# A log-sum-exp kernel on one core: six large loads issued in halves from two queues

## The chip, the cores and the metric

The kernel runs on one core of a Trainium2 chip. The metric is the device time of one execution in microseconds (us). The time before the change is the median of three runs, 162.56 us (162.5 to 163.04).

## What is computed

The input is a float32 array of 32 x 512 x 1024 numbers, normally distributed. For each of the 16384 rows of 1024 numbers the logarithm of the sum of the exponentials is taken, which leaves 32 x 512 numbers.

```python
def reference(x: np.ndarray, axis: int) -> np.ndarray:
    x_max = np.max(x, axis=axis, keepdims=True)
    return (x_max.squeeze(axis) + np.log(np.sum(np.exp(x - x_max), axis=axis))).astype(np.float32)
```

The kernel takes no maximum off: it computes log(sum(exp(x))) directly. The input is 67.1 MB, the output 64 KB.

## The kernel before

The 16384 rows are laid over the 128 partitions, 128 consecutive rows to each partition (`x_v`, L51). What a partition holds is worked off in 17 chunks of 4, 15, 16, 16, 16, 14, 13, 9, 7, 5, 4, 3, 2, 1, 1, 1 and 1 rows (`CHUNKS`, L11). A row of a partition is 4 KB, so a load of chunk 1 brings 60 KB into each of 128 partitions, and a load of chunks 2, 3 and 4 brings 64 KB.

The chunks land in a ring of 51 rows per partition (`ring`, L54). Chunks 0 to 3 fill it exactly (4 + 15 + 16 + 16). Chunk 4 starts at the front again, over chunks 0 and 1; chunk 5 lies over the end of chunk 1 and most of chunk 2; chunk 6 over the end of chunk 2 and the first half of chunk 3; chunk 7 over the first half of chunk 4, and so on.

All loads are issued by SyncE in the order of the chunks (`load`, L92 to L102). Ahead of a load that goes over used rows, SyncE waits until VectorE (`dve_done`) and, where needed, ScalarE (`act_done`) have finished with them. Chunk i has a semaphore of its own, `landed[i]`, which its load raises by 16. The load of chunk 0 is moved ahead of the first barrier (L184 to L192).

ScalarE works in the order of the program. It loads its table (L122); for every chunk it waits for `landed[i]` (L135), and takes Exp in place in one or two parts (L137). VectorE sums each part along its rows as soon as that Exp is done, with one reduction (L157), or row by row with a fused add of the row's two halves in chunks 8, 9, 10 and 12 (L144). In some chunks the last row, and in chunks 13 to 16 the only row, is summed by ScalarE itself while it takes Exp (L164). The logarithms are taken by ScalarE in three instructions (L108): for the first 81 rows per partition ahead of chunk 7, for the next 43 rows ahead of the last chunk's row, and for the last four at the end. Each waits for the sums that it reads. SyncE then stores the result (L176).

No scheduler orders the work: the order on each engine is that of the program text.

The softmax here doesn't subtract the row's maximum and nothing guards it: scores larger than these inputs give would overflow.

## Time and profile before

| what | value |
|---|---|
| median of three runs | 162.56 us |
| the profiled execution's own time | 162.84 us |
| span of its profile | 161.5 us |
| VectorE busy | 121.0 us (75% of the span) |
| ScalarE busy | 115.1 us (71%) |
| DMA packets' time, as a share of 16 engines' span | 97.3% |
| read from memory | 67.11 MB, mean 416 GB/s over the span |
| ScalarE's idle time until a load has landed | 43.9 us in 7 waits |
| VectorE's idle time until an Exp is done | 37.2 us in 4 waits |

The landings follow from the starts of ScalarE's Exps that waited for a load: chunk 0 at 7.44 us from the span's start, chunk 1 at 25.65, chunk 2 at 45.33, chunk 3 at 64.81, chunk 4 at 84.14, chunk 5 at 101.07 and chunk 6 at 116.83. After that ScalarE hardly waits. The span begins with SyncE's first issue, and the profiled execution's time is 1.3 us longer than its span. All numbers that are read from the profile are of that one execution.

To read the lines below: DVE is VectorE, ACT is ScalarE, SP (or SPq, its queue) is SyncE; L157 is line 157 of the kernel. A line of a timeline gives start and duration in us, engine, line, operation, output and input with their shapes, how many instructions were merged, and in brackets the idle time before the first and what ended it.

### The profile page before, as it was taken

The page shows a single profiled execution, that of the slowest core. Times are in us where ns is not written, and L with a number is a line of the kernel's source. Part 1 is how long each engine was busy: PE and PEld are TensorE (multiplying, and loading weights), DVE is VectorE, ACT ScalarE, POOL GpSimd, SP SyncE. Part 2 cuts the span into 40 slices and gives each one's busy share as a digit, 9 for nine tenths or more (in the row PEclk, how much of TensorE's full clock was granted, in tenths as well). Part 3 has the DMA queues.
Part 4 walks back from the last instruction along what each step waited for, and adds up shares of the span by engine and source line. Part 5 has one row for each costly group of instructions (what it writes and reads, how often), then busy time and mean ns, then how long its engine had stood idle before and what let it go on. Part 6 is the DMA issues. An engine that isn't in the chain of part 4 may idle for free.

```text
span 161.5 us, 126 instructions
## 1 busy us (share of the span) xinstructions
DVE 121.0 (75%) x46; ACT 115.1 (71%) x40; POOL 0.2 (0%) x4
## 2 busy tenths in 40 slices
DVE  0028000004999999999999599999999999999892
ACT  3170006995079960999519993999199999999995
POOL 0000000000000000000000000000000000000000
DMA  7999899989799799699799999999899999999991
GB/s 268 495 487 457 350 411 520 406 373 520 308 471 520 325 455 520 276 503 520 325 422 455 455 455 438 422 422 422 366 429 438 444 433 406 441 414 423 405 407 36
DMA packets 2592, 67.18 MB, mean 416 GB/s; under 512 B 288, under 2 KB 416, under 8 KB 928
## 3 DMA queue, kind: packets, MB, share of 16 engines
q1 hardware_dynamic: 2592, 67.18, 97.3%
HBM read 67.11 MB, written 0.07 MB: 416 GB/s over the span
## 4 chain that ended last, share of the span: by engine, by line
DMA 49%; DVE 29%; ACT 20%; issue 0%
DMA ring<-in_x_dram 49%; DVE sums L157 29%; ACT ring L137 17%; ACT ring L164 3%; ACT res L108 0%
## 5 line engine op out<-in xcount | busy, mean ns | idle before, releaser
L157 DVE TENSOR_REDUCE sums<-ring 128x8 f32<-128x8192 f32 (+5 forms) x14 | 111.2, 7995 | 37.4 <-ACT ring L137 37.2
L137 ACT ACTIVATE ring<-ring 128x8192 f32<-128x8192 f32 (+6 forms) x18 | 104.4, 5836 | 44.0 <-DMA ring<-in_x_dram 43.9
L144 DVE CUSTOM_DVE_ANT_0 ring<-ring 128x512 f32<-128x512 f32 x16 | 9.9, 688 | 0.0
L164 ACT ACTIVATE ring<-ring 128x1024 f32<-128x1024 f32 x9 | 9.3, 1042 | 0.0
L122 ACT ACT_TABLE_LOAD x1 | 1.3, 1283 | 0.8 <-PEq L209 0.8
L164 ACT ACTIVATION_READ_ACCUMULATOR ring<-ring 128x1 f32 x9 | 1.6, 173 | 0.0
L144 DVE DVE_READ_ACCUMULATOR2_ANT sums<- 128x1 f32 x16 | 1.4, 85 | 0.0
L108 ACT ACTIVATE res<-sums 128x81 f32<-128x81 f32 (+1 forms) x2 | 0.5, 248 | 0.0
L108 ACT ACTIVATE res<-late 128x4 f32<-128x4 f32 x1 | 0.2, 173 | 0.0
L209 POOL MEMSET const-bfloat16-1.0<- 128x1 bf16 x1 | 0.1, 102 | 0.0
L209 POOL MEMSET const-uint8-127<- 128x1 uint8 x1 | 0.1, 102 | 0.0
L209 POOL MEMSET const-float32-0.0<- 128x1 f32 x1 | 0.1, 99 | 0.2 <-issue 0.2
L209 POOL MEMSET const-float32-1.0<- 128x1 f32 x1 | 0.1, 99 | 0.0
## 6 DMA issues: line engine op xcount, KB each, us to landing
ring<-in_x_dram SPq DMA_DIRECT2D x1, 7680.0 KB, 24.8
ring<-in_x_dram SPq DMA_DIRECT2D x1, 7168.0 KB, 29.0
ring<-in_x_dram SPq DMA_DIRECT2D x1, 6656.0 KB, 36.2
ring<-in_x_dram SPq DMA_DIRECT2D x1, 4608.0 KB, 20.3
ring<-in_x_dram SPq DMA_DIRECT2D x2, 2048.0 KB, 16.1
ring<-in_x_dram SPq DMA_DIRECT2D x1, 3584.0 KB, 28.4
ring<-in_x_dram SPq DMA_DIRECT2D x1, 2560.0 KB, 27.4
ring<-in_x_dram SPq DMA_DIRECT2D x4, 512.0 KB, 27.1
```

Source lines behind the costliest of these rows:

```text
L108: nc.scalar.activation(out=res[:, lo:hi], in_=src, func=Ln).then_inc(act_done, 1)
L122: nc.scalar.preload_act_table_set("natural_log_exp_and_others")
L137: nc.scalar.activation(out=ring[:, s + lo : s + hi], in_=ring[:, s + lo : s + hi], func=Exp).then_inc(act_done, 1)
L144: nc.vector.tensor_tensor_reduce(out=ring[:, s + j, : D // 2], in0=ring[:, s + j, : D // 2], in1=ring[:, s + j, D // 2 :], scale=1.0, scal ...
L157: nc.vector.reduce_sum(out=sums[:, row + lo : row + hi], in_=ring[:, s + lo : s + hi], axis=AX).then_inc(dve_done, 1)
L164: nc.scalar.activation(out=ring[:, s + j], in_=ring[:, s + j], func=Exp, accum_out=total(row + j),).then_inc(act_done, 1)
L209: nc = _bacc.Bacc("TRN2", target_bir_lowering=False, num_devices=1)
```

## The change

Chunks 1 to 6 (`TWO_QUEUES`) are loaded by two transfers each: SyncE issues the 64 even partitions, ScalarE the 64 odd ones. A partition's piece is as large as before and contiguous as before. Both raise the chunk's semaphore by 16, so ScalarE waits for 32. The loads of chunk 0 and of chunks 7 to 16 stay whole on SyncE.

On ScalarE the three odd halves of chunks 1 to 3 are issued at the start, ahead of the table load. The odd half of chunk 4 is issued behind the Exps of chunk 2, that of chunk 5 behind those of chunk 3, and that of chunk 6 behind those of chunk 4. ScalarE makes the same waits ahead of them as SyncE makes ahead of the even halves: for chunk 4 on the sum of chunk 1, for chunk 5 on the second sum of chunk 2, for chunk 6 on the first sum of chunk 3. SyncE's order of loads is unchanged.

```diff
+TWO_QUEUES = range(1, 7)
...
-    def load(i):
+    def fetch(engine, i, first=0, step=1):
         (s, row), r = place[i], CHUNKS[i][0]
         act_wait = max(a for a, _ in busy[s : s + r])
         dve_wait = max(d for _, d in busy[s : s + r])
         if dve_wait:
-            nc.sync.wait_ge(dve_done, dve_wait)
+            engine.wait_ge(dve_done, dve_wait)
         if act_wait:
-            nc.sync.wait_ge(act_done, act_wait)
-        nc.sync.dma_start(out=ring[:, s : s + r], in_=x_v[:, row : row + r]).then_inc(
-            landed[i], 16
-        )
+            engine.wait_ge(act_done, act_wait)
+        engine.dma_start(
+            out=ring[first:P:step, s : s + r], in_=x_v[first:P:step, row : row + r]
+        ).then_inc(landed[i], 16)
+
+    def load(i):
+        if i in TWO_QUEUES:
+            fetch(nc.sync, i, 0, 2)
+        else:
+            fetch(nc.sync, i)
...
+    for i in range(1, 4):
+        fetch(nc.scalar, i, 1, 2)
     nc.scalar.preload_act_table_set("natural_log_exp_and_others")
...
-        nc.scalar.wait_ge(landed[i], 16)
+        nc.scalar.wait_ge(landed[i], 32 if i in TWO_QUEUES else 16)
...
         done_before.append((dves, acts))
+        if i + 2 in TWO_QUEUES and i + 2 > 3:
+            fetch(nc.scalar, i + 2, 1, 2)
```

## The prediction, made before the changed kernel was run

> **What bounds the kernel now.** I read the page first (engine shares, the 40 slices), then the busy time by stretch, then the two compute engines' timelines, then SyncE's waits and issues.

> ```profile
> DVE  0028000004999999999999599999999999999892
> DMA  7999899989799799699799999999899999999991
> q1 hardware_dynamic: 2592, 67.18, 97.3%
> DMA packets 2592, 67.18 MB, mean 416 GB/s; under 512 B 288, under 2 KB 416, under 8 KB 928
> ```

> One queue carries everything, and its 16 DMA engines are hardly ever without work. The packet counts give the descriptor: 17 loads of 128 partitions are 2176 packets, the store is 128, and 288 under 512 B are 18 transfers times 16 completion writes; the sum is 2592. So a packet here is one partition's row of one load (15 x 4 KB = 60 KB in load 1, 64 KB in loads 2 to 4), and each engine has 8 of them per load. The mean rate hides nothing in the middle. A line of the next view is a stretch, its length, busy DVE, ACT, POOL, the clock, the DMA share and GB/s; I cut at the landings of loads 0 to 6.

> ```profile
> 7.44:25.65 18.21, 4.42 (x1) 3.62 (x2) 0.00 (x0) 1.00 1.02 435
> 25.65:45.33 19.68, 6.65 (x1) 13.01 (x2) 0.00 (x0) 1.00 1.00 426
> 45.33:64.81 19.48, 19.48 (x3) 13.94 (x2) 0.00 (x0) 1.00 1.00 431
> 64.81:84.14 19.33, 19.33 (x3) 13.95 (x3) 0.00 (x0) 1.00 0.99 427
> 116.83:159.86 43.03, 40.39 (x37) 42.88 (x27) 0.00 (x0) 1.00 0.94 401
> ```

> Two facts. The DMA already moves 426 to 435 GB/s through the large loads, with a share of 0.99 to 1.02. And in the last 43 us ACT is busy 42.88: from load 6's landing at 116.83 ACT is the bound too, with the transfers ending just ahead of it (the last lands at 158.5, its Exp starts at 158.56). VectorE is the third limit:

> ```profile
> 11.09 4.42 DVE L157 TENSOR_REDUCE sums<-ring 128x4 f32<-128x4096 f32 x1 [11.09 <-ACT ring L137]
> 38.68 50.52 DVE L157 TENSOR_REDUCE sums<-ring 128x15 f32<-128x15360 f32 x5 [23.18 <-ACT ring L137]
> 91.20 53.00 DVE L157 TENSOR_REDUCE sums<-ring 128x8 f32<-128x8192 f32 x7 [1.99 <-ACT ring L137]
> ...
> 153.75 3.35 DVE L157 TENSOR_REDUCE sums<-ring 128x3 f32<-128x3072 f32 x1 [0.97 <-ACT ring L137]
> ```

> From 38.68 us, when load 1's sum starts, VectorE has only two gaps until its last sum at 158.3: 1.99 and 0.97 us. The end then follows ScalarE's L108 (waits for those sums), one row and one L108, to 159.86. Load 1's landing at 25.65 sets the start: 13.0 us of Exp, then 38.68. So a later load 1 has 2.0 + 1.0 us of free play, plus some 0.1 at the end, together 3.1 us, and beyond that the end moves one for one. SyncE's side is looser:

> ```profile
> SPq L100 <- DVE sums L157: 123.0, 7, 52.4
> 54.86 0.33 SPq L100 DMA_DIRECT2D ring<-in_x_dram  x1
> ```

> Load 4 is issued at 54.86, 9.95 us before load 3 has landed (64.81); an issue takes 0.33 us.

> [...] The trace has one queue; its issues take 0.33 to 0.75 us, so there is next to nothing to save. [...] No trace here shows two busy queues; this is the step on which my number rests. [...]

> **The change, part by part.** Instructions: ScalarE gains six DMA issues (three ahead of its table load, one each behind the Exps of chunks 2, 3 and 4) and three waits on sums; SyncE keeps 17 issues. Six issues at 0.33 to 0.75 us are 2 to 4.5 us of ScalarE's sequencer. The first three fall in the 5.38 us that ACT idles before load 0; the others ahead of waits of 5.38, 2.80 and 3.51 us for loads 4, 5 and 6. Cost nothing; without that cover 0.33 us each. No issue falls in the ACT-bound last 43 us.

> The bytes do not change, nor the descriptors. The gain has a ceiling: loads 2 and 3 took 19.68 and 19.48 us against 18.21 x 16/15 = 19.42 at load 1's rate, so perfect overlap of two queues returns some 0.3 us over the large loads; below nothing, the same amount could be lost in switching. I take 0.

> What moves is the order of packets. Before, load 0's 8 rows per engine go first, then load 1's 8. Now ScalarE's queue offers load 1's odd rows from about the first barrier on (SyncE's second issue is at 0.78; the first packets ran 1.0 us after the first issue, so 1.8 at the earliest), then those of loads 2 and 3, with nothing to hold them back. If an engine alternates packet by packet, every 16 KB row of load 0 left over is followed by a 60 or 64 KB row that is not yet needed. Costs: a 60 KB row is 18.21/8 = 2.28 us, a 64 KB row about 19.6/8 = 2.45, a 16 KB row 2.28 x 16/60 = 0.61. Load 0's last row ended near 7.0 before. ScalarE's rows join with n of load 0's rows left: n = 7 if they come at 1.8, n = 4 if they take some 1.5 to 2 us longer. I take 6, since an engine's first row started at 1.0 to 1.9 and takes over 0.6 us at the start.
> - Load 0: 7.0 + 4 x 2.28 + 2 x 2.45 = 21.0. Its Exp and sum (3.6 and 4.4 us) have time until load 1.
> - Load 1's even rows alternate with four 64 KB rows: 4 x (2.28 + 2.45) = 18.9, so 39.9, and landed about 40.2: 14.5 us later than 25.65.
> - VectorE starts load 1's sum at 40.2 + 13.0 = 53.2 and is then never short of work, since loads 2 and 3 still land near 54 and 65 (the sum of bytes is the same). It ends 14.5 - 3.1 = 11.4 us later.
> - The waits: load 4's both halves need load 1's sum, done at 53.2 + 16.2 = 69.4, while the DMA runs dry at 64.8: some 5 to 6 us of empty DMA, and load 4 lands near 90. ScalarE waits in line for that sum too (behind Exp of chunk 2, ending near 68.5) and then holds chunk 3's Exp for 1 us; behind chunk 3 it waits for chunk 2's second sum (53.2 + 16.2 + 17.3 = 86.7), ahead of load 4's landing. Queued behind it are only Exps whose sums VectorE reaches later. ACT's last stretch then starts 6 us late, inside VectorE's 11.4.
> Sum: 162.84 (this execution's own time; span 161.5) + 11.4 = 174.2; its own time stands 0.28 above the median 162.56, so about 174.0. With n = 4, load 1 lands 9.8 us late: +6.7, 169.2. With n = 7: 17.0 late, +13.9, 176.5.

> **The rivals.**
> 1. Fair sharing by bytes. If an engine mixes both queues finely, n = 6 rows of load 0 take twice 6 x 0.61, landing 3.7 us later, and ScalarE's queue stays 1.6 MB (3.7 us) ahead. Load 1 lands 3.3 to 4 us late; after the 3.1 us of play the end moves 0.2 to 0.9: about 163.1. For it: the slices show even flow. Against: the records are whole rows, one after the other.
> 2. Not slower: whole shares. An engine stays with one transfer's rows until its completion write, then changes queue. [...] Then load 0 is finished first, odd and even of load 1 follow, and all six landings stand: 162.6, or 162.3 with the 0.3 us gained. It decides from the point where load 1 lands by 28.7 (25.65 + 3.1). Against it: the profile counts each row as a packet.
> 3. [...] the six loads (109.4 us from 7.44 to 116.83) could take up to twice that: some 270. [...]
> 4. The change doing little because the later three halves come late from ScalarE: load 6's odd half is issued only behind chunk 4's Exps. It is still ahead of load 5's landing, so nothing by itself.

> **How the numbers follow.** Packet by packet 0.57; bytes 0.17; whole shares 0.14; a small gain 0.04; [...] another loss 0.04. The forecast is 174.0. What a measurement of this kernel can tell from no change is about 0.3% (0.5 us). Half of the byte case falls within it: same 0.14 + 0.08, slower 0.57 + 0.09 + 0.04 + 0.04, faster 0.04. The likeliest case alone spans 168.5 to 177; to leave out less than 2 in 10 the range must take in bytes and whole shares: 162.4 to 177. [...]

> **What would show it.** Right: ACT's first Exp starts near 21 instead of 7.44, its second near 40; VectorE's 128x15 sum starts near 53 and runs without a gap to about 170; load 4 is issued near 69 with an empty slice in the DMA row; GB/s elsewhere near 430. Wrong: load 1 landed by 29 (rivals 1, 2), or GB/s near 220 in the first slices (rival 3), or a gap in VectorE after load 1.

## The result, and the profile after

The changed kernel took 169.07 us (168.94 to 169.26, four runs) against 162.66 us (162.5 to 163.04, four runs) for the kernel before: a ratio of 1.039, 95% interval 1.037 to 1.041. It is slower by 6.4 us. The forecast was 174.0 with a range of 162.4 to 177.0. The profiled execution took 169.06 us with a span of 167.7, against 162.84 and 161.5 before.

The page of the changed kernel, lines of the 40 slices and of the DMA queues:

```profile
DVE  0000180000049999999999999999999999999992
DMA  7989998998999797699989999999899999999920
q1 hardware_dynamic: 2208, 43.58, 61.5%
q10 hardware_dynamic: 480, 23.59, 32.6%
```

There are two queues now. ScalarE's (q10) carries six transfers of 64 rows and 16 completion writes each (records of 4 bytes, as many to a transfer as the page counts DMA engines), 6 x 80 = 480 packets, so a packet is still one partition's row, or one such write. VectorE's row is the one that changed: its run of nines starts two slices later, then has no weak spot, and goes on to the end, while the DMA row has already fallen to 2 and 0.

Three stretches of the same kernel: between the landings of loads 0 and 1, between those of loads 1 and 2, and from load 6's landing on (stretch, length, busy DVE, ACT, POOL, clock, DMA share, GB/s):

```profile
16.49:35.24 18.75, 4.42 (x1) 3.62 (x2) 0.00 (x0) 1.00 1.01 437
35.24:54.68 19.44, 6.41 (x1) 13.00 (x1) 0.00 (x0) 1.00 1.01 432
119.91:166.08 46.17, 44.63 (x38) 42.99 (x27) 0.00 (x0) 1.00 0.88 372
```

While both queues have rows the rate is 437 and 432 GB/s, as with one queue (435 and 426 before). So the bytes flow as before; what they belong to has changed. And in the last stretch VectorE, not ScalarE, is busy nearly throughout.

The timeline of the changed kernel shows what became late; ahead of it stands the line of the kernel before for load 1:

```profile
25.65 13.00 ACT L137 ACTIVATE ring<-ring 128x15360 f32<-128x15360 f32 x1 [14.59 <-DMA ring<-in_x_dram]
```

```profile
0.78 2.27 ACTq L102 DMA_DIRECT2D ring<-in_x_dram  x3
16.49 3.62 ACT L149 ACTIVATE ring<-ring 128x4096 f32<-128x4096 f32 x1 [12.12 <-DMA ring<-in_x_dram]
35.24 13.00 ACT L149 ACTIVATE ring<-ring 128x15360 f32<-128x15360 f32 x1 [15.13 <-DMA ring<-in_x_dram]
48.27 103.21 DVE L169 TENSOR_REDUCE sums<-ring 128x15 f32<-128x15360 f32 x12 [23.72 <-ACT ring L149]
54.68 13.95 ACT L149 ACTIVATE ring<-ring 128x8192 f32<-128x8192 f32 x2 [6.45 <-DMA ring<-in_x_dram]
64.46 0.50 ACTq L102 DMA_DIRECT2D ring<-in_x_dram  x1
87.22 7.03 ACT L149 ACTIVATE ring<-ring 128x8192 f32<-128x8192 f32 x1 [4.75 <-DMA ring<-in_x_dram]
```

Load 0 lands at 16.49 instead of 7.44, load 1 at 35.24 instead of 25.65, load 2 at 54.68 instead of 45.33. Load 3 is complete at 64.57 by its semaphore, in time: the same bytes have arrived by then, but those of load 3 were mixed in among those of loads 0 to 2. VectorE's 128x15 sum starts at 48.27, 9.59 us late, and the 103.21 us after it have no gap. Before, they had gaps of 1.99 and 0.97 us. Load 4 is issued at 64.46, when load 1's sum is done, just after the engines have run out of rows: in the DMA records (the single packets of the same profile, with queue, size, start and duration of each) the last row of load 3 ends at 64.23, and the first of load 4 starts at 65.71.

VectorE's waits in the changed kernel (in total, times, longest):

```profile
DVE sums L169 <- ACT ring L149: 43.9, 2, 23.7
```

Before it was 37.2 us in 4 waits. The two that are left are those ahead of its first two sums; 43.9 - 37.2 = 6.7 us is about the loss.

### The profile page after: what moved, and what is told of

Same layout as the page of the kernel before. It is cut to its first block, busy times and chain, and to the rows that moved or that the text cites. A ratio compares the mean times of both kernels' runs of the same rounds, so it can differ in the third digit from the quotient of the medians.

```text
span 167.7 us, 132 instructions
## 1 busy us (share of the span) xinstructions
DVE 120.7 (72%) x46; ACT 115.1 (69%) x40; POOL 0.2 (0%) x4
## 2 busy tenths in 40 slices
DMA packets 2688, 67.18 MB, mean 401 GB/s; under 512 B 384, under 2 KB 512, under 8 KB 1024
## 4 chain that ended last, share of the span: by engine, by line
DVE 69%; DMA 21%; ACT 9%; issue 0%; ACTq 0%
DVE sums L169 64%; DMA ring<-in_x_dram 21%; ACT ring L149 8%; DVE ring L156 6%; ACT ring L176 1%; ACT res L116 0%; DVE sums L156 0%; ACTq L115 0%
## 5 line engine op out<-in xcount | busy, mean ns | idle before, releaser
L169 DVE TENSOR_REDUCE sums<-ring 128x8 f32<-128x8192 f32 (+5 forms) x14 | 111.0, 7992 | 43.9 <-ACT ring L149 43.9
L149 ACT ACTIVATE ring<-ring 128x8192 f32<-128x8192 f32 (+6 forms) x18 | 104.3, 5834 | 44.9 <-DMA ring<-in_x_dram 44.8
```

The costliest lines, as they stand in the source:

```text
L149: nc.scalar.activation(out=ring[:, s + lo : s + hi], in_=ring[:, s + lo : s + hi], func=Exp).then_inc(act_done, 1)
L169: nc.vector.reduce_sum(out=sums[:, row + lo : row + hi], in_=ring[:, s + lo : s + hi], axis=AX).then_inc(dve_done, 1)
```

## The experiments

All are edits of the changed kernel (for act_zero: of the kernel before); "..." in an edit stands for lines left out. "Theory A" is that of the prediction: engines take turns between the queues row by row, and what is late is late because the other queue's rows went ahead. The kernel before was timed beside each group, at 162.63, 162.26 and 162.38 us.

### One part of the change alone

later: loads 1 to 3 whole on SyncE, loads 4 to 6 split.

```diff
-TWO_QUEUES = range(1, 7)
+TWO_QUEUES = range(4, 7)
...
-    for i in range(1, 4):
-        fetch(nc.scalar, i, 1, 2)
```

> Only loads 4 to 6 are split; load 1 to 3 stay whole on SyncE. Theory A (the loss is the order of packets at the start: ScalarE's rows of loads 1 to 3 go ahead of load 1's even rows): load 1 lands at 25.6 us and the time is 162.4 to 163.1. Theory B (a good part of the loss comes with splitting as such: two queues taking turns, ScalarE's three waits on sums in mid-kernel): 164 to 166.

early: loads 1 to 3 split, loads 4 to 6 whole.

```diff
-TWO_QUEUES = range(1, 7)
+TWO_QUEUES = range(1, 4)
```

> Only loads 1 to 3 are split; loads 4 to 6 are whole on SyncE again. Theory A: load 1 lands at 35.2 as in the changed kernel and the time is 168.7 to 169.4. Theory B: 165 to 167, the part that the complement does not show.

Measured: early 169.11 us, ratio 1.040 (1.038 to 1.041), the whole loss, as theory A had it. But later took 167.68 us, ratio 1.032 (1.030 to 1.034), where theory A had 162.4 to 163.1, and theory B 164 to 166. Both missed. The parts do not add: one alone costs 6.5 us, the other 5.1, both together 6.4. The timeline of later says why:

```profile
25.53 13.00 ACT L147 ACTIVATE ring<-ring 128x15360 f32<-128x15360 f32 x1 [14.51 <-DMA ring<-in_x_dram]
54.74 0.56 ACTq L102 DMA_DIRECT2D ring<-in_x_dram  x1
71.61 7.03 ACT L147 ACTIVATE ring<-ring 128x8192 f32<-128x8192 f32 x1 [12.78 <-DMA ring<-in_x_dram]
78.67 17.28 DVE L167 TENSOR_REDUCE sums<-ring 128x8 f32<-128x8192 f32 x2 [6.77 <-ACT ring L147]
```

Loads 1 and 2 land in time (25.53 and 44.88). At 54.74 ScalarE issues load 4's odd half, while SyncE's queue still holds load 3's last rows. From 58.8 on these take turns, and load 3 lands at 71.61 instead of 64.81. In the DMA records, on the engines that end last, three rows of 2.42 us went ahead: two ahead of load 3's last two rows and one ahead of its completion write. That is 7.3 us, less the 0.45 by which load 2 was earlier in this run. VectorE waits 6.77 us for load 3, and 1.19 for load 4. It is the same overtaking at another place. In the changed kernel it does not happen there, because load 4 is issued at 64.46, when load 3 is complete. So theory A's expectation fell, since it looked for the mechanism only at the start; whether the mechanism or the splitting is to blame is what the next run tells.

### The halves without a second queue

same_queue: the same halves, both issued by SyncE, one behind the other.

```diff
         if i in TWO_QUEUES:
             fetch(nc.sync, i, 0, 2)
+            fetch(nc.sync, i, 1, 2)
...
-    for i in range(1, 4):
-        fetch(nc.scalar, i, 1, 2)
...
-        if i + 2 in TWO_QUEUES and i + 2 > 3:
-            fetch(nc.scalar, i + 2, 1, 2)
```

> All six loads are split in even and odd halves, but SyncE issues both, one behind the other, so that nothing overtakes. Theory A (the loss is overtaking between queues, splitting is free): landings as before (7.4, 25.6, 45.3, 64.8) and 162.3 to 163.1. Theory B (halves, twice the transfers, completion writes): 164 or more.

Measured: 162.42 us, ratio 1.000 (0.999 to 1.001). VectorE's timeline in same_queue:

```profile
38.51 50.52 DVE L168 TENSOR_REDUCE sums<-ring 128x15 f32<-128x15360 f32 x5 [23.08 <-ACT ring L148]
90.69 52.98 DVE L168 TENSOR_REDUCE sums<-ring 128x8 f32<-128x8192 f32 x7 [1.66 <-ACT ring L148]
```

The sums start and the gap comes back as in the kernel before. Six further issues, 96 further completion writes and the stepped partitions cost nothing that can be measured (162.42 us against 162.38). So the 6.4 us come from issuing the odd halves on ScalarE's queue, not from the halves. That the three later issues and their waits add nothing in the changed kernel is shown by early, which does without them.

### Turns, row by row

one_whole: load 1 whole on SyncE, all else as in the change. There is one split load less, but ScalarE's queue starts with the 64 KB rows of load 2.

```diff
-TWO_QUEUES = range(1, 7)
+TWO_QUEUES = range(2, 7)
...
-    for i in range(1, 4):
+    for i in range(2, 4):
         fetch(nc.scalar, i, 1, 2)
```

> Load 1 whole on SyncE, loads 2 to 6 split, so one split load less. Theory A (engines take turns packet by packet, each ScalarE row of 64 KB delays what SyncE has queued): load 0 lands at 7.4 + 4 x 2.42 = 17.1, load 1 after 8 rows of 2.27 and the four rows of load 3 at 2.42, near 44.9; that is 19.3 later than before, less 3.1 of free play: about 179 (176 to 181). Theory B (the loss grows with the number of split loads): below 169.

Measured: 178.88 us, ratio 1.100 (1.098 to 1.102), with load 0 at 17.34 and load 1 at 45.15. In the timeline of one_whole:

```profile
17.34 3.62 ACT L149 ACTIVATE ring<-ring 128x4096 f32<-128x4096 f32 x1 [13.96 <-DMA ring<-in_x_dram]
45.15 26.84 ACT L149 ACTIVATE ring<-ring 128x15360 f32<-128x15360 f32 x3 [24.20 <-DMA ring<-in_x_dram]
58.18 103.21 DVE L169 TENSOR_REDUCE sums<-ring 128x15 f32<-128x15360 f32 x12 [32.78 <-ACT ring L149]
74.92 13.95 ACT L149 ACTIVATE ring<-ring 128x8192 f32<-128x8192 f32 x2 [2.93 <-DVE sums L169]
```

Counting rows had given 17.1, 44.9 and about 179; theory B fell by 10 us. The last line also shows the price of a wait in ScalarE's line: chunk 3's Exp waits 2.93 us for load 1's sum, on which load 4's odd half waits ahead of it. It costs nothing here, since VectorE has work.

act_zero: the kernel before, with load 0 alone issued by ScalarE.

```diff
-    def load(i):
+    def load(i, engine=None):
+        engine = engine or nc.sync
...
-        nc.sync.dma_start(out=ring[:, s : s + r], in_=x_v[:, row : row + r]).then_inc(
+        engine.dma_start(out=ring[:, s : s + r], in_=x_v[:, row : row + r]).then_inc(
...
-    load(0)
+    load(0, nc.scalar)
```

> The kernel before, with load 0 alone issued by ScalarE and the rest by SyncE. Asks whether transfers issued by ScalarE start later than SyncE's (3.7 to 4.4 us from issue to the first row in the runs so far, against 1.0 to 1.3). Theory Q (a ScalarE issue takes about 4 us to its first row): first rows of load 0 near 4.2 with load 1's rows from 2.0 in turn with them, load 0 lands at 26 to 28, load 1 near 25.5. Theory S (only a second queue beside a busy one starts late): load 0's first rows start near 1.1, and load 1's come some 4 us after their issue.

Measured in a single execution: 162.63 us. In the timeline of act_zero:

```profile
16.66 3.62 ACT L138 ACTIVATE ring<-ring 128x4096 f32<-128x4096 f32 x1 [14.47 <-DMA ring<-in_x_dram]
25.74 13.00 ACT L138 ACTIVATE ring<-ring 128x15360 f32<-128x15360 f32 x1 [5.46 <-DMA ring<-in_x_dram]
38.77 50.52 DVE L158 TENSOR_REDUCE sums<-ring 128x15 f32<-128x15360 f32 x5 [14.05 <-ACT ring L138]
```

Load 0 lands as late as in the changed kernel (16.66 against 16.49), load 1 in time, and nothing is lost: a load 0 that is late by itself, by 9 us, costs nothing here. And theory S held: the first rows of ScalarE's load 0 start at 1.13 to 1.84 us in the DMA records, those of SyncE's load 1, issued at 0.91, at 4.72 to 5.39. So the late start, 3.8 us after the issue for SyncE's queue here and 1.0 for ScalarE's (issued at 0.12), is that of the second queue, not of ScalarE.

### When the second queue joins

sp_waits: SyncE holds loads 1 to 3 until load 0 has landed.

```diff
+        if i == 1:
+            nc.sync.wait_ge(landed[0], 16)
         if i:
             load(i)
```

> SyncE waits for load 0 before it issues loads 1 to 3; ScalarE issues its odd halves at the start as in the changed kernel. Asks why ScalarE's first row came 4.1 us after its issue. Theory L1 (its descriptors wait behind those of SyncE's three issues of the same time): without these its first rows start near 2.0, six rows of load 0 are left, load 0 lands at 21 or later. Theory L2 (a new queue's first row takes some 4 us, or the engines have the next rows of load 0 taken up already): first row near 4.9 again, load 0 near 16.5.

act_first: ScalarE issues load 1's odd half ahead of the first barrier.

```diff
     load(0)
+    fetch(nc.scalar, 1, 1, 2)
     n_early = len(body.instructions)
...
-    for i in range(1, 4):
+    for i in range(2, 4):
         fetch(nc.scalar, i, 1, 2)
```

> ScalarE issues the odd half of load 1 ahead of the first barrier, right beside SyncE's load 0. Theory L2a (a fixed start of about 4.1 us): first row near 4.1, one more row of load 0 behind it, load 0 near 18.7, load 1 near 37.5, about 171.4. Theory L2b (rows of load 0 already taken up by the engines are what it waits behind, a number of rows): with both issued together it joins after the first or second row, load 0 near 23 to 25, load 1 near 42 to 44, 176 to 178.

Measured in a single execution each. In sp_waits (173.31 us) ScalarE's first rows start at 4.56 to 5.86, load 0 lands at 16.55: L1 fell, the even issues of the same time do not delay them. (Load 1 lands only at 39.48 there, because its even rows are issued only when load 0 has landed.) In act_first (169.01 us) the issue is at 0.12 and the first rows start at 4.53 to 5.18, behind five rows of load 0, where it was mostly five or six in the changed kernel; load 0 lands at 16.44 and load 1 at 35.19. Neither number of L2a or L2b came out; the start of L2a (4.4 us after the issue) did, but it fell on nearly the same row. From issue to the second queue's first row it was 3.7 us in hold_all below, 4.1 in the changed kernel and in later. What stays open is whether it is a time, or rows that an engine has taken up ahead: between the issue and the second queue's first row an engine served some five or six rows of 16 KB, or ended the row in hand and served one or two more of 60 or 64 KB. A fixed time would have to differ by 0.7 us between these runs, which speaks for the second without showing it.

### Holding ScalarE's rows back

hold_all: ScalarE waits for load 0 before its three early issues.

```diff
+    nc.scalar.wait_ge(landed[0], 16)
     for i in range(1, 4):
         fetch(nc.scalar, i, 1, 2)
```

> ScalarE issues its three early odd halves only when load 0 has landed (7.4). Theory A: load 0 at 7.4; ScalarE's first row starts between 8.7 (issue plus some 1.2 us) and 12 (issue plus the 4.1 us that the changed kernel showed), then four rows and a completion write take turns with SyncE's rows: load 1 lands at 27 to 31, 1.4 to 5.4 later than before, so the time is 162.6 to 165. Theory B (splitting as such): near 169.

hold_two: ScalarE issues the odd halves of loads 2 and 3 when load 1 has landed.

```diff
-    for i in range(1, 4):
-        fetch(nc.scalar, i, 1, 2)
+    fetch(nc.scalar, 1, 1, 2)
...
         nc.scalar.wait_ge(landed[i], 32 if i in TWO_QUEUES else 16)
+        if i == 1:
+            fetch(nc.scalar, 2, 1, 2)
+            fetch(nc.scalar, 3, 1, 2)
```

> All six loads split, but ScalarE issues the odd halves of loads 2 and 3 only when load 1 has landed. Theory A: load 0 still lands near 16.5, load 1 at 25.7, load 2 near 47 to 52 instead of 45.3 (its odd rows then alternate with SyncE's), load 3 at 64.8; VectorE has the slack for it: 162.6 to 163.6. Theory B (the late load 0, or the alternation as such, costs): 165 to 169.

hold_early: hold_two's edit, and loads 4 to 6 whole.

```diff
-TWO_QUEUES = range(1, 7)
+TWO_QUEUES = range(1, 4)
```

> As hold_two, but loads 4 to 6 whole on SyncE. Theory A (the 3 us that hold_two kept come from load 4's odd rows, which went ahead of load 3's last rows; load 3 landed at 69.5): load 3 lands at 64.8 again, VectorE waits some 1.2 us at load 2 and hardly elsewhere, 162.4 to 163.3. Theory B (the late load 2, at 50.2, is what costs): 165 to 166.

Measured: hold_all 163.87 us, ratio 1.009 (1.007 to 1.012), load 1 at 30.20, within theory A. hold_two 165.68 us, ratio 1.018 (1.017 to 1.020): load 0 at 16.43, load 1 at 25.7, load 2 at 50.19 as counted, but load 3 at 69.52 instead of 64.8, so theory A's time missed. hold_early 163.65 us, ratio 1.007 (1.005 to 1.009), between the two theories, with load 3 still late. Load 3's Exp and VectorE's sums in hold_two, then in hold_early:

```profile
69.52 7.03 ACT L151 ACTIVATE ring<-ring 128x8192 f32<-128x8192 f32 x1 [5.38 <-DMA ring<-in_x_dram]
39.94 16.15 DVE L171 TENSOR_REDUCE sums<-ring 128x15 f32<-128x15360 f32 x1 [15.44 <-ACT ring L151]
57.25 17.28 DVE L171 TENSOR_REDUCE sums<-ring 128x8 f32<-128x8192 f32 x2 [1.16 <-ACT ring L151]
76.58 17.28 DVE L171 TENSOR_REDUCE sums<-ring 128x8 f32<-128x8192 f32 x2 [2.05 <-ACT ring L151]
95.34 52.78 DVE L171 TENSOR_REDUCE sums<-ring 128x8 f32<-128x8192 f32 x7 [1.48 <-ACT ring L151]
```

```profile
68.96 13.95 ACT L151 ACTIVATE ring<-ring 128x8192 f32<-128x8192 f32 x2 [5.41 <-DMA ring<-in_x_dram]
56.66 17.28 DVE L171 TENSOR_REDUCE sums<-ring 128x8 f32<-128x8192 f32 x2 [0.65 <-ACT ring L151]
76.02 69.97 DVE L171 TENSOR_REDUCE sums<-ring 128x8 f32<-128x8192 f32 x9 [2.08 <-ACT ring L151]
```

Load 4's odd rows were named as the cause of the late load 3; hold_early issues load 4 whole from SyncE and load 3 still lands at 68.96. There it is SyncE's queue that had run ahead: with ScalarE's halves held back, it came to load 4's rows (issued at 56.03) while load 3's odd half was still waiting its turns; the DMA records show the two taking turns until 68.5. So the queue that was held back was overtaken in its turn here: load 3 came at 68.96 instead of 64.81. VectorE's last wait for a large load ends at 95.34 in hold_two, with load 4's sum next; in hold_early load 4's sum follows load 3's at once, at 76.02 + 17.28 = 93.30. These 2.0 us are the difference of the two times: 1.48 is the wait for load 4, and the rest load 3's earlier landing.

In both runs ScalarE's two issues also stand between load 1's landing and its Exp, which starts 1.2 us later for it (26.91 and 26.82 instead of 25.7 and 25.6). It costs nothing here, since VectorE then waits for load 2 and load 3 all the same.

### Neighbouring partitions instead of every second one

halves: the same six loads, SyncE taking partitions 0 to 63 and ScalarE 64 to 127.

```diff
-    def fetch(engine, i, first=0, step=1):
+    def fetch(engine, i, first=0, n=128):
...
         engine.dma_start(
-            out=ring[first:P:step, s : s + r], in_=x_v[first:P:step, row : row + r]
+            out=ring[first : first + n, s : s + r], in_=x_v[first : first + n, row : row + r]
         ).then_inc(landed[i], 16)
...
-            fetch(nc.sync, i, 0, 2)
+            fetch(nc.sync, i, 0, 64)
...
-        fetch(nc.scalar, i, 1, 2)
+        fetch(nc.scalar, i, 64, 64)
```

The later three issues are changed in the same way.

> The same six loads, SyncE taking partitions 0 to 63 and ScalarE 64 to 127 instead of even and odd. Theory A (order of packets alone[...]): within 1 us of the changed kernel, 168 to 170. Theory C [...]: a 60 KB row takes up to 4.5 us instead of 2.27 while only one queue has rows, and the time is anywhere from 175 to 270.

Measured: 278.68 us, ratio 1.721 (1.711 to 1.731). Theory A fell; theory C had the kind right, and the time is 9 us past its range. In halves, by stretch between the landings of loads 0 to 3:

```profile
28.65:66.59 37.94, 4.42 (x1) 3.61 (x1) 0.00 (x0) 1.00 1.01 216
66.59:105.84 39.25, 16.15 (x1) 13.00 (x2) 0.00 (x0) 1.00 1.00 214
105.84:140.41 34.57, 17.28 (x2) 13.95 (x3) 0.00 (x0) 1.00 1.00 212
```

The DMA share is 1.00 and the rate is half: 216, 214 and 212 GB/s against 437 and 432 in the even and odd cut. Theory C had looked for slow rows only while one queue has rows; in the DMA records a 64 KB row takes 4.9 us at the median here, against 2.42 in the changed kernel, also at times when ten engines are on one queue's rows and six on the other's. Why a row takes twice as long with this cut is not shown: how the rows are dealt to the engines was not seen. The rates and the rows' durations are what was measured.

## Why the prediction was right, and what was off

The way it moved and the mechanism came as forecast, the size did not: a loss of 11.4 us was forecast and 6.4 came. The stated range held three of the prediction's cases, so that the time lies in it says little; what tells these cases apart is the landings.

**What one sum explains.** In every run the time follows VectorE: the start of its 128x15 sum plus the gaps that it has from there on. The time is that of the profiled execution. It is an account and not a test: it says that VectorE's own work from that start on is the same everywhere and ends the kernel; which landing made a start or a gap late is read from the timelines.

| run | start + gaps, us | time, us | time less start and gaps |
|---|---|---|---|
| before | 38.68 + 2.96 | 162.84 | 121.2 |
| changed | 48.27 + 0 | 169.06 | 120.8 |
| one_whole | 58.18 + 0 | 178.96 | 120.8 |
| sp_waits | 52.52 + 0 | 173.31 | 120.8 |
| hold_all | 43.24 + 0 | 164.03 | 120.8 |
| later | 38.56 + 7.96 | 167.51 | 121.0 |
| hold_two | 39.94 + 4.69 | 165.69 | 121.1 |
| hold_early | 39.85 + 2.73 | 163.57 | 121.0 |

The runs left out of the table (early, same_queue, act_first, act_zero and halves) leave 120.8 to 121.4.

- **Slower, and by load 1's delay less VectorE's play: right.** The play was put at 3.1 us. Among the runs without gaps it is 9.59 - 6.22 = 3.4 in the changed kernel (6.22 = 169.06 - 162.84), and 3.4 again in one_whole (19.50 - 16.12), sp_waits (13.84 - 10.47) and hold_all (4.56 - 1.19). Where the 0.3 us more come from was not followed up.
- **Turns packet by packet: right.** A turn is one recorded packet, and that is one row of 16 to 64 KB or one completion write: in the DMA records of the changed kernel rows of the two queues follow each other one by one. With records joined end to start, one engine that ends last starts a row of ScalarE's at 4.88 us, then one of SyncE's at 7.15, and so in turn at 7.75, 10.02, 10.62, 12.89 and 13.50, and the completion write of load 0 at 15.76. Ahead of that run this step was an assumption. Load 0's eight rows and its write did not go as one turn, so whole shares fell. Both rivals fell with the landings as well: whole shares would have left load 1 at 25.65; sharing by bytes had it 3.3 to 4 us late, and it was 9.6.
- **The term that was mis-sized: n.** Six rows of load 0 were expected to be overtaken. ScalarE's first rows started at 4.88 to 5.95 us, 4.1 us after their issue, where 1.0 was taken as the earliest and 1.5 to 2 more as the other bound. Load 0's landing was pushed back by four rows: 7.44 + 4 x 2.27 = 16.52, measured 16.49. In the DMA records of the engines that end last these are three ahead of a row of load 0 and one ahead of its completion write, which took a turn of its own (one row of ScalarE's from 13.50 to 15.76, then the write); the sum had left that out. So n was three, and there was one turn that had not been counted. From there the second step is exact: 4 x (2.27 + 2.42) = 18.76 gives 35.25, measured 35.24. The prediction's own line for n = 4 was 169.2; that it comes so near is in part luck, since three rows and one write make four turns too.
- **Load 4 and the dry DMA: right in kind, smaller.** It was issued at 64.46 (predicted 69.4) against load 3's landing at 64.57; in the DMA records an engine is without a row for 2.3 us on average, where 5 to 6 were forecast. Load 4 landed at 87.22, 3.1 us later than before, instead of near 90. It never reached VectorE, which had work.
- **ScalarE's six issues and three waits cost nothing: right for this kernel.** early shows it of the three later ones, since without them the time is the same (169.11); the three at the start end at 3.05, far ahead of load 0's landing. Chunk 3's Exp was not held for 1 us either: the sum that load 4 waits for was ready at 64.46, before chunk 2's Exps were done near 68.6. one_whole shows that hold, 2.93 us.
- **No gain in rate: right.** 437 and 432 GB/s where 435 and 426 were before.
- **A rate of half (the third rival): set aside rightly.** It had 0.04 and some 270 us; the even and odd cut kept 437 and 432 GB/s. halves shows what two queues on the two halves of the partitions cost: 212 to 216 GB/s and 278.68 us.

No run beat the kernel before; the nearest, same_queue, equals it.

## What to carry to other kernels

Before splitting a load over two queues, write down which rows the engines will serve in which order: here the queue with transfers issued far ahead took every second turn from what was needed first, and the larger its rows, the more time each turn took (2.27 us for 60 KB, 2.42 for 64 KB). One queue alone moved 426 to 435 GB/s here, a second one brought no rate (432 to 437), and its order would have had to be held by hand. Look for the engine whose work starts with the delayed load: if that engine's work ends the kernel, as VectorE's does here, the loss is the delay less that engine's later gaps (here 6.22 us of loss from 9.59 of delay), however busy the DMA stays.
